# Loading the attention's query tiles ahead, giving out twenty portions of the gate projection first, and padding the compressed values to 128 rows

## The chip, the cores and the metric

The kernel runs on one core of a Trainium2 chip. The metric is the device time of one execution in microseconds (us). Before the change the median of three runs is 1509.44 us (1508.98 to 1510.2). A core has TensorE (PE, matrix products; PEld is its loading of weights), VectorE (DVE), ScalarE (ACT), GpSimd (POOL) and a queue engine (SP) that issues most of the transfers between main memory and the core's own memory.

## The reference

One layer of a decoder with parallel mixers, on 1024 positions of width 1024, all float32:

```python
h = rms_norm(x, norm_mix)
proj = h @ w_in
q_flat, kv_flat, g_attn, u_pool, g_merge = split(proj, ...)
a = nsa_attention(q_flat, kv_flat, g_attn, ...) @ w_branch_attn
b = pool_mixer(u_pool, pool_w, pool_scale) @ w_branch_pool
ga, gb = split(sigmoid(g_merge), 2)
x = x + (ga * a + gb * b) @ w_out
h = rms_norm(x, norm_mlp)
return rms_norm(x + square(relu(h @ w_ff1)) @ w_ff2, norm_final)
```

The attention has 8 heads of 64 in two groups and three branches: over 63 compressed blocks of keys and values, over selected blocks (all 16 blocks are selected, so this is causal attention over everything), and over a window of 512. The three results are added with a sigmoid gate each.

## The kernel before

**Numbers in two parts.** Every large product is made of three: each operand is split into a rounded part (`hi`) and the rest (`lo`), and `mm3` (lines 74 to 79) issues hi·hi, hi·lo and lo·hi. A weight tile comes by SP into `wraw`, ACT rounds it into `whi`, and POOL or DVE subtracts to get `wlo` (`load`, lines 163 to 184).

**Stages.** First keys, values and queries are projected; the query tiles are written to main memory as `qd`, one per 128 positions. Then the pooling branch and its gate are made (lines 424 to 505; the tiles `gbd` go to main memory). Then comes the attention (from line 508), then the output projections, then a feed-forward part.

**The attention.** It goes through 32 pairs: 8 tiles of 128 positions (`i`), and for each 4 pairs of heads (`hp`). A query tile is loaded by `load_q`, for four heads at a time, and `split_q` turns it by four transposes on PE into `qh` and `ql`. For each pair there are two halves. The first (`units_a`) makes the scores on PE (`psS`), the maximum on DVE, the exponential on ACT, and scales the result (`pS` for the compressed block's 64 columns and the selected ones behind them, `pW` for the window). The second (`units_b`) turns the weights back by transposes (`psT`), two blocks of 128 at a time; ACT rounds them (`ph`), DVE subtracts (`pl`), and PE multiplies with the values into `oacc`. The values of the selected and window branches are `vst`, 128 rows; those of the compressed branch are `vch`, 64 rows, and its product is the last block of each pair. The second half of one pair is woven into the first half of the next.

**What fills PE meanwhile.** Another projection, the gate of the attention branch (`ga_terms`), is cut into 128 portions of one `mm3` (three products of 512 columns, into the one buffer `psG`; eight portions make a tile `z`, and a weight column block `m` serves 16). `advance` gives them out in proportion to the work done:

```python
while given < nterm and given < nterm * done / total:
    next(fill, None)
```

**What sets the order.** The code's order is a wish: a scheduler of the tile framework sets each engine's order from it and from the dependencies, so portions and transposes may stand earlier than where the code writes them. An engine then runs its row in order. Memory of a closed pool is used again, and a tile that lies in it waits for the last reader. The query tiles `qi` lie in the attention's own pool `wkB`, which takes over memory of the pooling stage. Beside this, POOL issues sums of feed-forward weights in main memory, one for each step of the attention's progress.

Of the kernel before, what the change touches and what calls it, by code (L numbers as in the profile page):

```python
# [8 lines left out]
F32 = mybir.dt.float32  # L9
F32R = mybir.dt.float32r  # L10
# [7 lines left out]
P = 128  # L18
# [4 lines left out]
HALF = 512  # L23
NH = 8
DH = 64
NG = 2
NCB = 64
# [22 lines left out]
def build(tc, a, out, dbg=None):  # L50
    nc = tc.nc
# [3 lines left out]
    def f(ap):  # L55
        return ap.bitcast(F32)
# [129 lines left out]
    vk = pool(attn, "vk")  # L186
    vst = [vk.tile([P, NT, NG, P], F32R, name=f"vst{b}") for b in range(2)]
    vch = vk.tile([DH, NG, P], F32R, name="vch")
    kds = vk.tile([P, NG, NCB + S], F32R, name="kds")
    kdw = vk.tile([P, NG, S], F32R, name="kdw")  # L190
    qd = [dram.tile([P, 2 * NH * DH], F32, name=f"qd{t}") for t in range(NT)]
# [89 lines left out]
    with ExitStack() as st:  # L281
# [4 lines left out]
        def compress(kv):  # L286
# [61 lines left out]
            else:  # L348
# [6 lines left out]
                for g in range(NG):  # L355
                    nc.vector.tensor_copy(vch[:, g], f(vh[g * DH:(g + 1) * DH]))

# [63 lines left out]
    blkctx.close()  # L421


    with ExitStack() as st:
# [6 lines left out]
        with ExitStack() as st2:  # L431
# [45 lines left out]
            for m in (3, 2, 1, 0):  # L477
                cur = pool_in(m)
                if prev is not None:
                    pool_mix(*prev)  # L480
                prev = cur
            for m in range(NK):
                if made:
# [27 lines left out]
    with ExitStack() as st:  # L511
        wk = pool(st, "wkB")
# [12 lines left out]
        def ga_terms():  # L525
            for m in range(NK):
                gh, gl = load(cols(a["w_in"], C_GA + m * P, P))
                for hf in range(2):
# [10 lines left out]
                    yield  # L539

        def load_q(i, g):
            qi = wk.tile([P, HALF], F32, name="qi", bufs=2)
            nc.sync.dma_start(qi, qd[i][:, g * HALF:(g + 1) * HALF])
            return qi

# [90 lines left out]
        def units_b(u):  # L636
            i, hp, g, nw, w0 = (u[n] for n in ("i", "hp", "g", "nw", "w0"))
            blocks = [(u["pS"], NCB + b * P, vst[0][:, b, g], P) for b in range(i + 1)]
            blocks += [(u["pW"], b * P, vst[1][:, w0 + b, g], P) for b in range(nw // P)]
            blocks.append((u["pS"], 0, vch[:, g], NCB))  # L640
            o = oacc[:, hp % 2]
# [4 lines left out]
            def tr(gi):  # L646
                bl = groups[gi]
                n = len(bl)
                ps = psT.tile([P, HALF], F32, name="psT").rearrange("p (b e n) -> p b e n", b=2, e=2)
                for j, (src, c0, _, _) in enumerate(bl):  # L650
                    for e in range(2):
                        nc.tensor.transpose(ps[:, j, e], src[e][:, c0:c0 + P], ident)  # L652
                ph = wk.tile([P, 2, 2, P], F32R, name="ph", bufs=3)
                pl = wk.tile([P, 2, 2, P], F32R, name="pl", bufs=3)
                nc.scalar.copy(ph[:, :n], ps[:, :n])  # L655
                nc.vector.tensor_tensor(pl[:, :n], ps[:, :n], f(ph[:, :n]), op=SUB)  # L656
                parts[gi] = (ph, pl)

            def pv(gi):
                ph, pl = parts.pop(gi)  # L660
                for part in (ph, pl):
                    for j, (_, _, v, rows) in enumerate(groups[gi]):
                        nc.tensor.matmul(o, lhsT=v, rhs=part[:rows, j], start=gi == 0 and j == 0 and part is ph,  # L663
                                         stop=2 * gi + j == nb - 1 and part is pl)
# [16 lines left out]

        LAG = 1
        fill = ga_terms()
# [5 lines left out]
        def advance(w):  # L689
            nonlocal done, given  # L690
            done += w
            while given < nterm and given < nterm * done / total:
                next(fill, None)
                given += 1

        qi = load_q(0, 0)
        q = split_q(qi)
        qnext = load_q(0, 1)
        bseq, bw = [], 0
# [42 lines left out]
        dump("oT", oT)  # L742
    psTctx.close()
    attn.close()

# [287 lines left out]
```

## Time and profile before

| | |
|---|---|
| median of three runs | 1509.44 us |
| the profiled execution | 1510.39 us, of it a span of 1508.6 us from the first to the last instruction |
| PE busy in the span | 1451.2 us (96%) |
| DVE, ACT, POOL busy | 66%, 50%, 12% |
| TensorE clock granted, mean | 0.981 |
| the attention | from 341.1 to about 708 us of the span |

All times below are of the profiled execution, in us from the start of its span. PE's times are starts and modelled ends, and products overlap their neighbours; so what a product costs is read from the distance of two starts, not from its length.

### The profile page before, as it was taken

How to read it: one execution, taken by the hardware profiler on the slowest of the kernel's cores; microseconds unless marked ns; L12 is line 12 of the kernel's file. 1: busy time of each engine (PE TensorE's matmuls, PEld its weight loads, DVE VectorE, ACT ScalarE, POOL GpSimd, SP SyncE). 2: the span in 40 equal slices, each digit the busy share in tenths (PEclk: the TensorE clock that was granted, in tenths of full speed). 3: DMA queues.
4: the chain of work that ended last, by engine and by line, in shares of the span. 5: the costliest groups of instructions: out<-in, count | busy, mean ns of one | idle time of the engine just before them, and what ended most of it. 6: DMA issues, size and time to landing. Idle time of an engine off the chain costs nothing.

```text
span 1508.6 us, 20793 instructions
## 1 busy us (share of the span) xinstructions
PE 1451.2 (96%) x7369; PEld 1199.6 (80%) x7369; DVE 1001.3 (66%) x1928; ACT 760.6 (50%) x1561; POOL 187.6 (12%) x238
## 2 busy tenths in 40 slices
PE   8999999997999999999899999999999999999995
PEld 6788888886788878787687888888888888888874
DVE  5693451115888888777648368667897386679974
ACT  4454231115877877765334353674344545754441
POOL 2006323330111111110010100000000000001021
PEclk9999999998999999999999999999999999999997
DMA  8234217875668777867944333333332223332312
GB/s 304 70 99 148 70 49 192 213 191 147 179 162 201 177 184 178 196 157 188 323 136 147 113 91 98 96 93 97 98 98 92 97 86 103 98 98 84 109 53 112
DMA packets 130201, 204.67 MB, mean 136 GB/s; under 512 B 9904, under 2 KB 62896, under 8 KB 129584
## 3 DMA queue, kind: packets, MB, share of 16 engines
q1 hardware_dynamic: 112032, 136.22, 28.8%
q0 software_dynamic: 17920, 67.11, 19.5%
q8 instruction: 58, 0.95, 0.3%
q14 instruction: 47, 0.39, 0.1%
q10 hardware_dynamic: 144, 0.00, 0.0%
HBM read 186.52 MB, written 83.89 MB: 179 GB/s over the span
## 4 chain that ended last, share of the span: by engine, by line
PE 84%; DVE 6%; DMA 5%; ACT 3%; issue 1%; POOL 1%; SPq 0%; POOLq 0%; DVEq 0%; ACTq 0%
PE psm L78 16%; PE psm L77 16%; PE psm L79 16%; PE oacc L663 5%; PE psF L78 5%; PE psF L79 5%; PE psF L77 5%; PE psT L652 4%; PE psS L557 3%; PE psS L558 2%; PE psG L77 2%; PE psG L78 2%; PE psG L79 2%; DMA xt<-in_x 1%; PE psS L560 1%
## 5 line engine op out<-in xcount | busy, mean ns | idle before, releaser
L78 PE MATMUL psm<-mv,whi 128*128 128x512 f32 x896 | 351.5, 392 | 0.0
L79 PE MATMUL psm<-mv,wlo 128*128 128x512 f32 x896 | 351.3, 392 | 0.0
L77 PE MATMUL psm<-mv,whi 128*128 128x512 f32 x896 | 351.2, 392 | 0.0
L82 DVE TENSOR_TENSOR wlo<-wraw,whi 128x512 fp32r<-128x512 f32 x288 | 198.8, 694 | 98.8 <-ACT whi L866 70.2
L866 ACT CAST whi<-wraw 128x512 fp32r<-128x512 f32 x224 | 138.8, 620 | 247.8 <-PE psm L78 185.5
L78 PEld LDWEIGHTS psm<-mv,whi 128*128 128x128 f32 x896 | 168.7, 188 | 37.0
L77 PEld LDWEIGHTS psm<-mv,whi 128*128 128x128 f32 x896 | 168.7, 188 | 36.9
L79 PEld LDWEIGHTS psm<-mv,wlo 128*128 128x128 f32 x896 | 168.7, 188 | 36.6
L179 ACT CAST whi<-wraw 128x512 fp32r<-128x512 f32 x112 | 69.7, 622 | 124.5 <-PE psF L78 58.0
L762 POOL TENSOR_TENSOR sqa<-sqa,sq 128x512 f32<-128x512 f32 x24 | 33.4, 1392 | 734.3 <-ACT sq L758 734.3
L656 DVE TENSOR_TENSOR pl<-psT,ph 128x512 fp32r<-128x512 f32 (+1 forms) x160 | 102.0, 647 | 30.3 <-ACT ph L655 29.0
L655 ACT CAST ph<-psT 128x512 fp32r<-128x512 f32 (+1 forms) x160 | 87.8, 556 | 49.0 <-PE psT L652 47.2
L567 DVE TENSOR_REDUCE nm<-psS 128x1 f32<-128x64 f32 (+8 forms) x192 | 100.0, 540 | 17.2 <-PE psS L560 10.1
L82 POOL TENSOR_TENSOR wlo<-wraw,whi 128x512 fp32r<-128x512 f32 x48 | 65.6, 1368 | 108.1 <-ACT whi L179 88.2
L78 PE MATMUL psF<-xl,whi 128*128 128x512 f32 x192 | 74.7, 389 | 0.0
L77 PE MATMUL psF<-xh,whi 128*128 128x512 f32 x192 | 74.7, 389 | 0.0
L79 PE MATMUL psF<-xh,wlo 128*128 128x512 f32 x192 | 74.7, 389 | 0.0
L568 ACT ACTIVATE pS<-psS,nm 128x64 f32<-128x64 f32 (+8 forms) x128 | 68.0, 533 | 8.8 <-DVE nm L567 8.3
L846 ACT CAST mv<-mt 128x512 fp32r<-128x512 f32 x96 | 59.1, 617 | 20.0 <-DVE mt L844 15.5
L82 DVE TENSOR_TENSOR mv<-mt,mv 128x512 fp32r<-128x512 f32 x96 | 67.3, 708 | 1.1 <-ACT mv L846 0.6
L663 PE MATMUL oacc<-ph,vst 128*128 128x256 f32 x264 | 64.1, 318 | 1.2 <-ACT ph L655 0.9
L652 PE MATMUL psT<-cf,pS 128*128 128x128 f32 x352 | 60.4, 276 | 2.8 <-DVE pS L624 2.6
(242 smaller groups left out, 3034.7 us busy)
## 6 DMA issues: line engine op xcount, KB each, us to landing
wraw<-wsw_ff SPq DMA_DIRECT2D x128, 256.0 KB
wraw<-in_w_ff SPq DMA_DIRECT2D x96, 256.0 KB
wsw_ff<-in_w_ff POOLq DMA_DIRECT2D x16, 1024.0 KB, 9.4
wsw_ff<-wsw_ff POOLq DMA_DIRECT2D x16, 1024.0 KB, 9.3
wraw<-in_w_in SPq DMA_DIRECT2D x40, 256.0 KB
wraw<-in_w_out SPq DMA_DIRECT2D x32, 256.0 KB
xt<-in_x SPq DMA_DIRECT2D x8, 512.0 KB
qd<-q SPq DMA_DIRECT2D x16, 256.0 KB
```

Of the source, the lines that this page charges most:

```text
L77: nc.tensor.matmul(ps, lhsT=sh, rhs=mh, start=first and i == 0, stop=False, skip_group_check=more)
L78: nc.tensor.matmul(ps, lhsT=sh, rhs=ml, start=False, stop=False, skip_group_check=more)
L79: nc.tensor.matmul(ps, lhsT=sl, rhs=mh, start=False, stop=last and i == n - 1, skip_group_check=more)
L82: eng.tensor_tensor(lo, src, f(hi), op=SUB)
L179: nc.scalar.copy(h, v)
L567: nc.vector.tensor_reduce(nm, v, axis=AX.X if flat else AX.XY, op=MAX, negate=True)
L568: nc.scalar.activation(p if flat else p.rearrange("p (a n) -> p a n", a=2), v, AF.Exp, bias=nm, accum_out=sm)
L652: nc.tensor.transpose(ps[:, j, e], src[e][:, c0:c0 + P], ident)
L655: nc.scalar.copy(ph[:, :n], ps[:, :n])
L656: nc.vector.tensor_tensor(pl[:, :n], ps[:, :n], f(ph[:, :n]), op=SUB)
L663: nc.tensor.matmul(o, lhsT=v, rhs=part[:rows, j], start=gi == 0 and j == 0 and part is ph, stop=2 * gi + j == nb - 1 and part is pl)
L866: nc.scalar.copy(hi, raw)
```

## The change

- `vch` gets 128 rows; the lower 64 are set to zero once, at the start, by POOL. The products with it take all 128 rows of `ph` and `pl` instead of 64.
- The query tiles `qi` get a pool of their own, `qp`, opened behind the query projection; it has two buffers, as before. The first two tiles are loaded by code that stands in front of the loop over the pooling branch's gate.
- `advance` gives out 20 portions at its first call, and the other 108 in proportion to the work done.

```diff
-    vch = vk.tile([DH, NG, P], F32R, name="vch")
+    vch = vk.tile([P, NG, P], F32R, name="vch")
+    nc.gpsimd.memset(f(vch[DH:P]), 0.0)
...
+    qctx = ExitStack()
+    qp = pool(qctx, "qp")
+
+    def load_q(i, g):
+        qi = qp.tile([P, HALF], F32, name="qi", bufs=2)
+        nc.sync.dma_start(qi, qd[i][:, g * HALF:(g + 1) * HALF])
+        return qi
...
+            qi = [load_q(0, 0), load_q(0, 1)]
             for m in range(NK):
...
-            blocks.append((u["pS"], 0, vch[:, g], NCB))
+            blocks.append((u["pS"], 0, vch[:, g]))
...
-                        nc.tensor.matmul(o, lhsT=v, rhs=part[:rows, j], ...
+                        nc.tensor.matmul(o, lhsT=v, rhs=part[:, j], ...
...
-        LAG = 1
+        LAG, FIRST = 1, 20
...
-            while given < nterm and given < nterm * done / total:
+            while given < nterm and given < FIRST + (nterm - FIRST) * done / total:
...
-        qi = load_q(0, 0)
-        q = split_q(qi)
-        qnext = load_q(0, 1)
+        q = split_q(qi[0])
+        qnext = qi[1]
```

**Where the first query tile is split.** PE's row at the start of the attention, in the kernel before: `psG` are the gate's portions, `cf,qi` the four transposes of the first query tile, `kds,qh` the first scores.

```order
L79 MATMUL psG<-xh_66,wlo 128x512
L77 MATMUL psG<-xh_67,whi 128x512
L78 MATMUL psG<-xl_75,whi 128x512
L549 MATMUL psT<-cf,qi 128x128 x4
L79 MATMUL psG<-xh_67,wlo 128x512
L77 MATMUL psG<-xh_68,whi 128x512
L78 MATMUL psG<-xl_76,whi 128x512
L79 MATMUL psG<-xh_68,wlo 128x512
L557 MATMUL psS<-kds,qh 128x192
```

In the changed kernel the same transposes stand in PE's row some 530 rows earlier, in the first step of the pooling branch's gate (`plh`, `mxh` are the pooled values):

```order
L77 MATMUL psF<-plh,pwh 128x512
L78 MATMUL psF<-pll,pwh 128x512
L79 MATMUL psF<-plh,pwl 128x512
L554 MATMUL psT<-cf,qi 128x128
L77 MATMUL psF<-mxh,whi 128x512
L554 MATMUL psT<-cf,qi 128x128 x3
L78 MATMUL psF<-mxl,whi 128x512
```

The transposes have moved out of the attention's start; they are the only PE work that went into the stage before.

**Where the twenty portions stand.** PE's row behind the first scores, in the changed kernel: `cf,pS` and `cf,pW` are the transposes of the first pair's weights. Ahead of these rows stand 24 products of the gate, behind them 24 more.

```order
L79 MATMUL psG<-xh_71,wlo 128x512
L77 MATMUL psG<-xh_72,whi 128x512
L78 MATMUL psG<-xl_80,whi 128x512
L79 MATMUL psG<-xh_72,wlo 128x512
L657 MATMUL psT<-cf,pS 128x128 x2
L657 MATMUL psT<-cf,pW 128x128 x2
L562 MATMUL psS<-kds,qh 128x192
L563 MATMUL psS<-kds,ql 128x192
L77 MATMUL psG<-xh_65,whi 128x512
```

In the kernel before the transposes of the first pair follow straight on the scores of the second:

```order
L557 MATMUL psS<-kdw,qh 128x128
L558 MATMUL psS<-kdw,ql 128x128
L652 MATMUL psT<-cf,pS 128x128 x3
L652 MATMUL psT<-cf,pW 128x128 x2
L652 MATMUL psT<-cf,pS 128x128
```

Up to the first pair's product with `vch` stand 6 portions before, and 22 now. In the 25 pairs behind it the counts are the same in both (88 portions). So the portions that moved to the front are missing in the last six pairs: 33.7 before, 17.7 now.

**The last pair.** PE's row at the end of the attention, in the kernel before:

```order
L652 MATMUL psT<-cf,pW 128x128 x4
L78 MATMUL psG<-xl_79,whi 128x512
L79 MATMUL psG<-xh_71,wlo 128x512
L663 MATMUL oacc<-ph,vst_98 128x256 x2
L663 MATMUL oacc<-pl,vst_98 128x256 x2
L652 MATMUL psT<-cf,pW 128x128 x2
L652 MATMUL psT<-cf,pS 128x128 x2
L77 MATMUL psG<-xh_72,whi 128x512
```

and in the changed kernel:

```order
L657 MATMUL psT<-cf,pW 128x128 x4
L668 MATMUL oacc<-ph,vst_98 128x256 x2
L668 MATMUL oacc<-pl,vst_98 128x256 x2
L657 MATMUL psT<-cf,pW 128x128 x2
L657 MATMUL psT<-cf,pS 128x128 x2
L668 MATMUL oacc<-ph,vst_98 128x256 x2
```

Nothing of the gate is left between the last pair's steps.

## Rows read from the trace of the kernel before

**Rows 1.** The page: busy time, share of the span and instructions of each engine.

```profile
PE 1451.2 (96%) x7369; PEld 1199.6 (80%) x7369; DVE 1001.3 (66%) x1928; ACT 760.6 (50%) x1561; POOL 187.6 (12%) x238
```

**Rows 2.** Busy us by engine, granted clock, DMA: first pair, next 25, last six.

```profile
341.10:361.90 20.80, 15.31 (x75) 12.66 (x75) 7.92 (x34) 8.17 (x34) 1.02 (x1) 0.75 0.48 128
361.90:618.50 256.60, 251.42 (x1648) 202.85 (x1647) 210.59 (x513) 199.86 (x524) 42.03 (x47) 1.00 0.74 180
618.50:708.20 89.70, 87.95 (x569) 72.76 (x568) 69.75 (x133) 62.91 (x132) 12.06 (x14) 1.00 0.72 168
```

**Rows 3.** Who waited for whom on PE, whole span: total, times, longest.

```profile
PE psT L549 <- DMA qi<-qd: 4.6, 1, 4.6
...
PE psm L79 <- DVE wlo L82: 2.7, 1, 2.7
```

**Rows 4.** Order of time, PE at the attention's start: start, length, instruction, idle before.

```profile
342.86 0.39 PE L78 MATMUL psG<-xl,whi 128*128 128x512 f32 x1
347.85 1.12 PE L549 MATMUL psT<-cf,qi 128*128 128x128 f32 x4 [4.60 <-DMA qi<-qd]
```

**Rows 5.** Order of time, SP's queue: pool weights, then the first query tile.

```profile
162.29 0.39 SPq L435 DMA_DIRECT2D s<-in_pool_w  x1
...
340.32 0.44 SPq L543 DMA_DIRECT2D qi<-qd  x1
```

**Rows 6.** Busy us by engine, then granted clock, behind the wait for the query tile.

```profile
345.00:352.00 7.00, 4.15 (x17) 3.73 (x17) 1.15 (x3) 0.78 (x2) 0.00 (x0) 0.53 0.75 257
352.00:359.00 7.00, 6.14 (x34) 5.18 (x34) 5.21 (x27) 5.90 (x29) 0.00 (x0) 0.74 0.00 1
```

**Rows 7.** Busy us of the gate's portions alone (PE, PEld, DVE): same stretches.

```profile
341.10:361.90 20.80, 8.15 (x21) 4.87 (x21) 0.00 (x0) 0.75 0.48 128
361.90:618.50 256.60, 85.94 (x264) 44.34 (x263) 7.52 (x11) 1.00 0.74 180
618.50:708.20 89.70, 31.84 (x100) 16.65 (x100) 3.42 (x5) 1.00 0.72 168
```

**Rows 8.** Order of time, PE: ordinary products of 128 rows, in the middle.

```profile
480.11 0.28 PE L663 MATMUL oacc<-ph,vst 128*128 128x256 f32 x1
480.23 0.40 PE L663 MATMUL oacc<-pl,vst 128*128 128x256 f32 x2
...
481.14 0.39 PE L77 MATMUL psG<-xh,whi 128*128 128x512 f32 x1
481.37 0.40 PE L78 MATMUL psG<-xl,whi 128*128 128x512 f32 x1
```

**Rows 9.** Order of time, PE: one product of 64 rows between products of 128.

```profile
548.59 0.29 PE L663 MATMUL oacc<-ph,vst 128*128 128x256 f32 x1
548.81 0.38 PE L663 MATMUL oacc<-ph,vch 64*128 64x256 f32 x1
549.12 0.50 PE L77 MATMUL psG<-xh,whi 128*128 128x512 f32 x1
549.46 0.39 PE L78 MATMUL psG<-xl,whi 128*128 128x512 f32 x1
```

**Rows 10.** Order of time, PE: two products of 64 rows side by side.

```profile
442.52 0.38 PE L663 MATMUL oacc<-ph,vch 64*128 64x256 f32 x1
442.75 0.27 PE L663 MATMUL oacc<-pl,vch 64*128 64x256 f32 x1
442.95 0.50 PE L77 MATMUL psG<-xh,whi 128*128 128x512 f32 x1
443.29 0.40 PE L78 MATMUL psG<-xl,whi 128*128 128x512 f32 x1
```

**Rows 11.** Busy us of the products with `vch` (PE, PEld, DVE): same stretches.

```profile
341.10:361.90 20.80, 0.50 (x2) 0.29 (x2) 0.00 (x0) 0.75 0.48 128
361.90:618.50 256.60, 15.41 (x50) 8.14 (x50) 0.00 (x0) 1.00 0.74 180
618.50:708.20 89.70, 4.06 (x12) 2.05 (x12) 0.00 (x0) 1.00 0.72 168
```

More of the change, by code (lines that the diff above doesn't have):

```diff
@@ L355, in compress @@
                 for g in range(NG):
-                    nc.vector.tensor_copy(vch[:, g], f(vh[g * DH:(g + 1) * DH]))
+                    nc.vector.tensor_copy(vch[0:DH, g], f(vh[g * DH:(g + 1) * DH]))
         def keys(t, br, dst):
@@ L539, in ga_terms @@
                     yield
[L541 to L544, printed above, removed]
         def split_q(qi):
@@ L637, in units_b @@
             i, hp, g, nw, w0 = (u[n] for n in ("i", "hp", "g", "nw", "w0"))
-            blocks = [(u["pS"], NCB + b * P, vst[0][:, b, g], P) for b in range(i + 1)]
-            blocks += [(u["pW"], b * P, vst[1][:, w0 + b, g], P) for b in range(nw // P)]
-            blocks.append((u["pS"], 0, vch[:, g], NCB))
+            blocks = [(u["pS"], NCB + b * P, vst[0][:, b, g]) for b in range(i + 1)]
+            blocks += [(u["pW"], b * P, vst[1][:, w0 + b, g]) for b in range(nw // P)]
+            blocks.append((u["pS"], 0, vch[:, g]))
             o = oacc[:, hp % 2]
@@ L649, in tr @@
                 ps = psT.tile([P, HALF], F32, name="psT").rearrange("p (b e n) -> p b e n", b=2, e=2)
-                for j, (src, c0, _, _) in enumerate(bl):
+                for j, (src, c0, _) in enumerate(bl):
                     for e in range(2):
@@ L661, in pv @@
                 for part in (ph, pl):
-                    for j, (_, _, v, rows) in enumerate(groups[gi]):
-                        nc.tensor.matmul(o, lhsT=v, rhs=part[:rows, j], start=gi == 0 and j == 0 and part is ph,
+                    for j, (_, _, v) in enumerate(groups[gi]):
+                        nc.tensor.matmul(o, lhsT=v, rhs=part[:, j], start=gi == 0 and j == 0 and part is ph,
                                          stop=2 * gi + j == nb - 1 and part is pl)
@@ L743, in build @@
     psTctx.close()
+    qctx.close()
     attn.close()
```

## The prediction

> **What bounds the kernel now.** I read the page's busy times first [rows 1]: PE is busy 96% of the span, the others at most 66%. So an edit counts for what it takes from PE's row, and for what it lets PE wait. Only the attention is touched. Its three stretches [rows 2] are the first pair, the 25 pairs behind it and the last six. In the middle PE is busy 251.4 of 256.6 us and in the last stretch 87.95 of 89.7; DVE, the next, has 82% and 78%. So PE is the bound there, with DVE not far behind. In the first stretch PE is busy only 15.3 of 20.8 us. The list of waits [rows 3] names the reason: 4.6 us for the first query tile, the longest wait there but for small ones on DVE and ACT.
>
> Busy isn't the same as useful, though, because products overlap. What one costs is the distance to the next start. An ordinary 128-row product of 256 columns takes 0.12 us (480.11 to 480.23), one of 512 columns 0.23 us (481.14 to 481.37) [rows 8]. A portion, three of the latter, is 0.69 us of PE.
>
> **Part 1, the query tile and the portions at the front.** Now the load goes out at 340.32, when SP comes to it [rows 5], and PE stops: starts at 342.86 and 347.85, 4.99 us apart where 0.23 would do, so 4.8 us lost [rows 4]. Then the granted clock is 0.53 and 0.74 in the next two stretches of 7 us [rows 6], so partly the lower level of 1.2 GHz instead of 2.4, after that stop and a sparse row of PE. The work done in 4.15 and 6.14 busy us would have taken 4.15 x 0.47 + 6.14 x 0.26 = 3.5 us less at the full level.
>
> After the change the load stands behind the query projection, about 180 us earlier, and the transposes stand in the pooling gate's first step, so the wait goes. What is late next is the rounding of `qh` and `ql` on ACT and DVE; one portion's product and some 0.5 us of waiting lie there, a small part of the rest below. The load takes SP's place in front of the pool weights [rows 5]; both wait for the same release of memory, and nothing queued behind them is needed within the microsecond that two more issues take. I cost that at nothing; if that cover fails, it is about 1 us. The added memset on POOL at the start is also nothing: POOL is 12% busy.
>
> The first stretch now holds 20.8 us = 4.8 of waiting + 3.5 of low clock + 7 portions (21 products in [rows 7]) of 0.69 = 4.8 + a rest of 7.7, in which PE also waits for the softmax of the first pair. PE's row after the change has 22 portions up to the same point: 15.2 us. The rest lies between 5 us (all its waits covered) and 7.7. I take 6.8 less 0.4 for the first pair's share of part 2: 21.6 us, +0.8 us. The bounds are -1 and +2. So the stretch stays as long, but takes 15 portions more with it.
>
> **Part 2, the padding.** The third timeline [rows 9] shows one product with the 64-row `vch`: the product ahead of it takes 0.22 instead of 0.12 us, it takes 0.31 instead of 0.12, and the 512-column one behind it 0.34 instead of 0.23. That is 0.10 + 0.19 + 0.11 = 0.40 us for one excursion to 64 rows. Two side by side [rows 10] take 0.23 and 0.20 and the one behind 0.34, which is 0.30, and with 0.10 for the one ahead again 0.40. There are 64 such products, 2, 50 and 12 by stretch [rows 11]. By PE's row, 18 pairs have their two side by side and 14 have them apart, so 18 + 28 = 46 excursions: 1 in the first stretch, 35 in the middle, 10 in the last. At 0.40 us that is 14.0 us in the middle and 4.0 in the last. A padded product is an instruction like the one with `vst`, and I take 0.12 us for it.
>
> The Trainium skill is of two minds here. "TensorE: Matmul & The Clock Gate" says under "What happens when you issue a matmul" that the time of a weight load goes by its columns and that the row count doesn't matter; by that the padding would change nothing, which is the second rival below. "TensorEngine Tiling (Array Packing)" says under "Key Properties" that a change of tiling mode drains the array, and 64 rows are such a mode; the delays on both sides of the 64-row product agree with this one.
>
> How much of it stays? In the middle nothing else changes: the same 88 portions stand in it. 256.6 - 14.0 = 242.6 us would put DVE, with 210.6 us of work, at 87%; it is at 82% now, while PE is the bound. I take 86% as what it reaches before PE loses time to it, so 210.6 / 0.86 = 244.9 us: **-11.7 us**. The bounds are -14.0 and, if DVE couldn't go over 82%, nothing.
>
> **Part 3, the last six pairs.** 16 portions fewer (33.7 against 17.7 by PE's rows; the 100 products in [rows 7] agree), 16 x 0.69 = 11.0 us, and 4.0 us of part 2: PE needs 74.7 us. DVE's 69.75 us lose two evictions of the gate (3.42 us for 5), so 68.4 us. That would be 92%; at 86% the stretch takes 79.5 us: **-10.2 us**. The bounds are -15.0 (no time lost to DVE) and 68.4 / 0.82 = 83.4 us, -6.3.
>
> **Behind the attention** nothing is edited, but it starts some 20 us earlier, with the same transfers in a shorter time (DMA share 0.72 to 0.74 now [rows 2]). PE waits there once for 2.7 us for a late weight tile [rows 3]; that wait may go or double, so 3 us either way, taken as 0.
>
> **Sum.** 0.8 - 11.7 - 10.2 = -21.1 us. The profiled execution took 1510.39 us, which gives 1489.3. The median of the runs lies 0.95 us under that execution, so **1488 us**.
>
> **The rivals.**
> - *DVE takes over.* PE waits little on DVE now only because PE is slow enough; with less fill between the steps of a pair, DVE's 82% is the ceiling. Against it: PE is busy for 98% of the middle, so the 82% is what PE leaves it. For it: the last pairs lose their fill altogether. Then the middle gains nothing and the last stretch 6.3: 0.8 - 6.3 = -5.5, 1504 us. Chance 14%.
> - *The padding does nothing*, that is, the delays belong to `vch`'s place at the end of a pair and not to its rows. For it: it is always the last block. Against it: also the product behind is late, where it is a gate portion that waits for nothing. Then 1.2 in front, 0 in the middle, and the last stretch's PE work is 78.7 us, still under 79.5 at 86%: -10.2. Together -9.0, 1500 us. Chance 7%.
> - *Slower: the last six pairs fall apart.* Without portions, transposes, rounding, subtraction and product of a pair follow each other, and PE and DVE work by turns. PE has 74.7 us there and DVE 68.4. The other parts give 10.9 us, so this decides, with 3 us more for a measurable loss, from the point where the stretch takes over 89.7 + 13.9 = 103.6 us: when 42% of DVE's work lies outside PE's. At half it is 108.9 us, +19.2 - 10.9 = +8.3 us: 1518 us. Against it: two `psT` buffers and the next pair's scores still overlap. Chance 4%.
>
> **How the numbers follow.** The forecast has 75%, the rivals 14, 7 and 4%. The range takes in the lowest sum (-1 - 14 - 15 = -30, 1479; with the part behind one way or the other it is rarely reached, so 1480) and reaches up to the second rival's 1500, at 1501; what is outside is most of the first and all of the third rival. A measurement of this kernel tells 0.2%, 3 us, from no change. Faster by more: the forecast, the second rival and nearly all of the first, 92%; within: a mixture of the first and third, 4%; slower: 4%.
>
> **What would show it.** In the profile after: no wait of PE for `qi`, and the granted clock at 1 from 341 us on; the first pair's end still at about 362 us. A `vch` product with a start distance of about 0.12 us, and its neighbours at theirs. The middle stretch at about 245 us with DVE at 86%, the last at about 80 us, PE waiting there for DVE or ACT. Wrong would be: a middle that is no shorter (first or second rival, told apart by the distances at `vch`), a last stretch over 90 us, or a front that is longer by several microseconds because PE waits for `qh` or for the portions' weights.

## The result, and the profile after

The changed kernel takes 1501.05 us (median of 6 runs, 1498.78 to 1505.85) against 1510.05 us for the kernel before on the same chip (6 runs, 1508.98 to 1511.78). The ratio is 0.9936, with a 95% interval of 0.992 to 0.9952: 9 us faster, 0.6%. The forecast was 22 us. The sign was right and the size was not: the time lies at the very top of the range, 0.05 us outside, and less than half of the forecast gain came.

The profiled execution has a span of 1497.0 us. First the page's busy times, which answer to [rows 1]:

```profile
PE 1439.9 (96%) x7369; PEld 1193.7 (80%) x7369; DVE 1001.6 (67%) x1928; ACT 760.4 (51%) x1561; POOL 188.9 (13%) x239
```

PE has 11.3 us less work, and its share is still 96%. The three stretches of [rows 2], now from 337.2 us on, with the same columns (busy us of PE, weight loads, DVE, ACT and POOL, then granted clock and DMA):

```profile
337.20:359.70 22.50, 21.61 (x120) 17.83 (x121) 9.72 (x35) 9.86 (x37) 3.56 (x3) 1.00 0.44 119
359.70:609.50 249.80, 243.82 (x1651) 199.89 (x1648) 211.28 (x513) 199.75 (x523) 42.77 (x47) 1.00 0.76 184
609.50:695.80 86.30, 78.80 (x520) 65.35 (x519) 68.21 (x132) 61.44 (x129) 9.87 (x12) 0.98 0.72 165
```

| stretch | before | forecast | after |
|---|---|---|---|
| first pair | 20.8 | 21.6 | 22.5 |
| next 25 pairs | 256.6 | 244.9 | 249.8 |
| last six pairs | 89.7 | 79.5 | 86.3 |
| the three together | 367.1 | 346.0 | 358.6 |

The attention lost 8.5 us. Behind it the kernel takes 0.8 us more. The stretch ahead of it is 3.9 us shorter in this execution, but that isn't the change: from 55 to 62 us the trace of before has a granted clock of 0.52, and this one has 1.00. The traces of the experiments show that dip in most cases and not in others, whatever the edit: of two executions of one and the same kernel, e3 has it and e9 has not.

The portions alone, as in [rows 7]: 22 in the first pair, 89 in the middle, 17 in the last six.

```profile
337.20:359.70 22.50, 16.38 (x66) 12.08 (x66) 1.38 (x2) 1.00 0.44 119
359.70:609.50 249.80, 84.39 (x266) 45.02 (x266) 7.48 (x11) 1.00 0.76 184
609.50:695.80 86.30, 16.25 (x52) 8.96 (x52) 2.06 (x3) 0.98 0.72 165
```

Two `vch` products side by side, in order of time on PE, at the place of [rows 10] (start, length, instruction):

```profile
437.15 0.48 PE L668 MATMUL oacc<-pl,vst 128*128 128x256 f32 x2
437.46 0.28 PE L668 MATMUL oacc<-ph,vch 128*128 128x256 f32 x1
437.58 0.28 PE L668 MATMUL oacc<-pl,vch 128*128 128x256 f32 x1
437.70 0.39 PE L77 MATMUL psG<-xh,whi 128*128 128x512 f32 x1
437.93 0.40 PE L78 MATMUL psG<-xl,whi 128*128 128x512 f32 x1
```

The distances are 0.12, 0.12 and 0.23 us, where [rows 10] has 0.23, 0.20 and 0.34: at this place the padding removed the 0.30 us that the prediction read there, and 0.09 more ahead of it. So the instructions became as fast as forecast. PE's waits within the attention (total, times, longest):

```profile
PE psT L657 <- DVE pS L629: 6.0, 9, 1.1
PE oacc L668 <- DVE pl L661: 2.7, 10, 0.5
PE psS L562 <- ACT pS L573: 1.7, 1, 1.7
PE oacc L668 <- ACT ph L660: 1.2, 3, 0.5
```

The 4.6 us for the query tile [rows 3] are gone. What is there instead is the pair itself: transposes that wait until DVE has scaled `pS`, products that wait for `pl`, scores that wait until ScalarE has read the last ones.

### The profile page after: what moved, and what is told of

Its sections match the earlier page's. It is cut to its first block, busy times and chain, and to the rows that moved or that the text cites. A ratio compares the mean times of both kernels' runs of the same rounds, so it can differ in the third digit from the quotient of the medians.

```text
span 1497.0 us, 20789 instructions
## 1 busy us (share of the span) xinstructions
PE 1439.9 (96%) x7369; PEld 1193.7 (80%) x7369; DVE 1001.6 (67%) x1928; ACT 760.4 (51%) x1561; POOL 188.9 (13%) x239
## 4 chain that ended last, share of the span: by engine, by line
PE 84%; DVE 8%; DMA 3%; ACT 3%; issue 1%; POOL 1%; SPq 0%; POOLq 0%; DVEq 0%; ACTq 0%
PE psm L78 16%; PE psm L77 16%; PE psm L79 16%; PE psF L78 5%; PE oacc L668 5%; PE psF L77 5%; PE psF L79 5%; PE psT L657 4%; PE psS L562 3%; PE psS L563 2%; PE psG L77 2%; PE psG L78 2%; PE psG L79 2%; DMA ta<-tad 1%; PE psS L565 1%
## 5 line engine op out<-in xcount | busy, mean ns | idle before, releaser
L179 ACT CAST whi<-wraw 128x512 fp32r<-128x512 f32 x112 | 69.7, 622 | 126.6 <-PE psF L78 56.9
L82 DVE TENSOR_TENSOR mv<-mt,mv 128x512 fp32r<-128x512 f32 x96 | 67.2, 707 | 1.1 <-ACT mv L851 0.6
```

What stands on the lines that cost most here:

```text
L82: eng.tensor_tensor(lo, src, f(hi), op=SUB)
L179: nc.scalar.copy(h, v)
```

## The experiments

All compare with the kernel before, measured beside them; there it took 1513.6 to 1514.3 us and not 1510, so the ratios are what to compare, not the times. Two theories went in. **A**: a pair has a length of its own, from the scores over maximum, exponential, scaling, transpose, rounding and subtraction to the products. PE's time saved below that length comes back as waits, and portions in it are free. **B**: DVE's throughput is the ceiling. A third, **C**, was that the padding does nothing. This table is worked out from the traces: portions are products of the gate by three, and the stretches end as those above do, where DVE begins the last addition of a pair's result (`oT`).

| kernel | portions | first pair | middle | last six | ratio, 95% interval |
|---|---|---|---|---|---|
| before | 7 / 88 / 33 | 20.8 | 256.6 | 89.7 | 1 |
| padding alone (e1) | 7 / 88 / 33 | 22.3 | 250.8 | 87.8 | 0.9940 (0.9925 to 0.9955) |
| tile ahead alone (e11) | 3 / 93 / 32 | 10.5 | 267.5 | 86.7 | 0.9975 (0.9964 to 0.9986) |
| tile ahead, 20 first (e2) | 22 / 89 / 17 | 22.5 | 256.9 | 90.7 | 0.9979 (0.9967 to 0.9990) |
| tile ahead, padding (e3) | 3 / 93 / 32 | 10.6 | 258.6 | 84.6 | 0.9908 (0.9894 to 0.9922) |
| the same again (e9) | 3 / 93 / 32 | 10.5 | 258.3 | 84.5 | 0.9910 (0.9893 to 0.9928) |
| tile ahead, padding, 8 first (e4) | 10 / 91 / 27 | 14.8 | 254.1 | 89.1 | 0.9931 (0.9913 to 0.9949) |
| the change: all, 20 first | 22 / 89 / 17 | 22.5 | 249.8 | 86.3 | 0.9936 (0.9920 to 0.9952) |
| the change again (e10) | 22 / 89 / 17 | 22.6 | 249.3 | 86.3 | 0.9922 (0.9906 to 0.9939) |

A kernel's stretches repeat to half a microsecond (e3 and e9, the change and e10).

One thing in the table misleads. At the end of the middle DVE's addition starts about 1 us behind the end of PE's last product in the other kernels of the table, but 4.2 to 5.5 us behind it in e3, e9 and e11, where it stands in DVE's queue behind work for later pairs. In e3 (start, length, instruction):

```profile
602.98 0.28 PE L668 MATMUL oacc<-pl,vch 128*128 128x256 f32 x1
608.72 0.28 DVE L674 TENSOR_TENSOR oT<-oacc,ot 64x128 f32<-64x128 f32 x1
```

So the table makes the middle of these three 3 to 4 us too long against the others, and their last six as much too short. Cut at the end of PE's last product of a pair instead, the middle and the last six are:

| kernel | portions, middle / last six | middle | last six |
|---|---|---|---|
| before | 88 / 33 | 256.9 | 89.9 |
| e1 | 88 / 33 | 251.1 | 88.0 |
| e11 | 90 / 35 | 264.8 | 90.4 |
| e2 | 89 / 17 | 257.5 | 90.9 |
| e3 | 90 / 35 | 255.2 | 89.0 |
| e9 | 90 / 35 | 255.9 | 87.8 |
| the change | 89 / 17 | 250.4 | 86.7 |

### Padding alone

```diff
-    vch = vk.tile([DH, NG, P], F32R, name="vch")
+    vch = vk.tile([P, NG, P], F32R, name="vch")
+    nc.gpsimd.memset(f(vch[DH:P]), 0.0)
...
-            blocks.append((u["pS"], 0, vch[:, g], NCB))
+            blocks.append((u["pS"], 0, vch[:, g], P))
```

> Padding alone. Theory A (the padding gives PE its 0.40 us per excursion, but the pairs hand part of it back in waits; the last pairs are bound by the length of their chain once they have no fill): the middle 25 pairs about 7 us shorter, as in the changed kernel, the last six pairs 2 to 4 us shorter because their portions are still there to fill the gaps; 1499 to 1502 us. Rival B (DVE is the ceiling of the middle at 82%): the middle stays at 256 us and the whole within 1508 to 1511. Rival C (the padding does nothing, the middle's gain in the changed kernel came from somewhere else, such as the clock or the order of the front): 1510, each vch product still 0.2 to 0.3 us.

Measured: ratio 0.9940, 1503.74 us. Its middle and last six, in the columns of [rows 2]:

```profile
359.90:610.70 250.80, 243.34 (x1647) 199.49 (x1646) 211.62 (x512) 200.08 (x523) 43.47 (x47) 1.00 0.76 184
610.70:698.60 87.90, 85.64 (x568) 71.71 (x567) 69.57 (x135) 63.04 (x133) 12.16 (x14) 1.00 0.74 169
```

C falls, and so does B in its strict form: the middle got 5.8 us shorter and DVE went from 82% to 84%. A had 7 us for the middle and 2 to 4 for the last six, where 1.9 came. The first pair got 1.5 us longer, since PE waits 6.3 us for the query tile here and not 4.6. This kernel's PE row stands in the same order as before's, so start distances can be compared instruction by instruction. In the middle the `vch` products with their neighbours on both sides take 10.7 us less. All the other instructions there take 5.0 us more: the transposes of `pS` 2.3 us, the products with `pl` 1.5, the scores most of the rest. 10.7 won on the spot, 5.0 handed back. The waits of PE in the middle show the same two names growing, before first (where `pl` has no row) and then with the padding:

```profile
PE psT L652 <- DVE pS L624: 2.0, 3, 1.1
```

```profile
PE psT L653 <- DVE pS L625: 2.9, 4, 1.1
PE oacc L664 <- DVE pl L657: 1.7, 2, 1.3
```

Over the whole kernel the excursions of which both traces have all records (46) gave 14.8 us on the spot, 0.32 us each in the mean (0.38 in the median) and not 0.40.

### The front without the padding

The changed kernel with the four lines on `vch` put back and `rhs=part[:v.shape[0], j]` in the product.

> The query tile ahead and twenty portions first, without the padding. Theory A: the first pair's stretch 22 to 23 us, 1 to 2 us longer than before; the middle unchanged at 256 us; the last six pairs, with 16 portions fewer, only 0 to 3 us shorter because the last pairs wait for their own chain: 1508 to 1511 us. Rival B (DVE throughput): the last six pairs get down to what DVE needs at 82 to 86%, 80 to 83 us, so 1502 to 1505. Rival C: the whole gain of the change is here, 1501.

Measured: 0.9979, 1511.57 us. The first pair's stretch is 22.5 us. The last six:

```profile
621.10:711.80 90.70, 84.67 (x521) 68.92 (x520) 68.38 (x132) 61.53 (x129) 9.19 (x12) 0.94 0.71 160
```

Here 16 portions, 11 us of PE's work, were taken out of a stretch in which PE was busy for 88 of 89.7 us [rows 2], and it became 1.0 us longer. Part of it is the clock: 10.2 us of the stretch ran at 0.50, where before has 1.00 throughout, so up to 5.1 us were lost that way. Even without them the stretch would have gained 4 us at most, and not 11. That refutes the third part of the prediction. Theory A's numbers hold but for this stretch, which it had 0 to 3 us shorter.

### Fewer portions first

```diff
-        LAG, FIRST = 1, 20
+        LAG, FIRST = 1, 0
```

(and 8 in the second kernel.)

> The changed kernel with no portions given out first (query tile ahead and padding stay); by PE's row 2.7 portions stand in the first pair, 90.5 in the middle and 35 in the last six. Theory A: a portion in front costs nearly its full 0.69 us there, and one in the last pairs costs nearly nothing, so without them the front takes 10 to 14 us instead of 22.5, the middle 251, the last six 86 to 88: 1491 to 1497 us, faster than the changed kernel. Rival B or C: the portions in front only fill its gaps; without them the front still takes 18 to 20 us and the last six pairs are back at 88 to 90: 1500 to 1504 us, no better than the changed kernel.

> The changed kernel with eight portions first instead of twenty: 10 in the first pair, 89.7 in the middle, 28.4 in the last six by PE's row. Theory A: front 14 to 17 us, middle 250 to 251, last six 85 to 87, so 1493 to 1498 us, between the kernel without any portions first and the changed one. Rival B or C: front 18 to 20, last six 84 to 88: 1499 to 1503 us.

Measured: 0.9908 (1500.44 us) and 0.9931 (1503.17 us). The kernel with none first:

```profile
339.50:350.10 10.60, 9.51 (x65) 7.55 (x65) 7.94 (x34) 7.78 (x34) 0.95 (x1) 1.00 0.95 211
350.10:608.70 258.60, 249.10 (x1669) 205.15 (x1668) 212.70 (x517) 201.88 (x526) 42.18 (x47) 0.99 0.74 179
608.70:693.30 84.60, 82.82 (x555) 69.87 (x554) 66.94 (x130) 60.83 (x130) 12.26 (x14) 1.00 0.73 172
```

In front A is right: 10.6, 14.8 and 22.5 us with 3.3, 10 and 22 portions, so a portion there costs 0.64 us. In the last six it is nearly right, cut at PE's last product: 35 portions and 89.0 us (87.8 in e9) against 17 and 86.7 in the changed kernel, so 18 portions, 12 us of PE's work, cost 1 to 2 us. But the middle was to be as long as the changed kernel's, and cut so it is 4.8 us longer. One or two portions more (0.9 us) and one stretch of low clock (at most 1.7) don't cover that. The rest goes with where the portions stand: in the last five pairs of the middle e3 has 27 and the changed kernel 20.7, and there e3 takes 69.7 us and the changed kernel 65.1. In the 20 pairs ahead of them e3 has 5 portions fewer, 3.4 us of PE's work, and is no shorter (185.5 and 185.3 us, with the low clock in it). So a portion can cost its full price in one pair and bring little when it is missing from another. With eight first the last six have 89.1 us at a clock of 0.96; there the forecast missed.

### No portions in the pairs

```diff
-        LAG, FIRST = 1, 20
+        LAG, FIRST = 1, 128
```

> The changed kernel with all 128 portions given out first, so that the last 25 pairs or so have no fill at all: what a pair takes when only its own chain and engines bound it. Theory A (the late pairs are bound by their chain): the last six pairs take as long without any of the changed kernel's 17 portions, 83 to 88 us, plus what a low granted clock adds, and 7-2 and 7-3 again 16 to 18 and 10 to 12 us; with 88 portions moved out of the middle, it gets shorter by much less than 88 x 0.69 = 60 us: 30 to 45, and the whole kernel is slower than the changed one, 1510 to 1535 us. Rival B' (PE's work bounds the pairs also without fill): the middle falls by 55 to 60 us, the last six to 75 to 78, the whole stays within 1495 to 1505 us.

Measured: 1567.07 us, ratio 1.034. All portions stand in the pairs of the first row of queries, up to 447.1 us. The 22 pairs behind them, and the last six:

```profile
447.10:678.40 231.30, 195.91 (x1299) 155.54 (x1298) 188.73 (x456) 176.86 (x453) 24.45 (x32) 0.97 0.65 156
678.40:762.60 84.20, 71.12 (x468) 57.18 (x466) 65.04 (x126) 57.84 (x123) 9.57 (x12) 0.96 0.65 153
```

The same 22 pairs with 83 portions in them, in the changed kernel, and in the kernel before:

```profile
375.30:609.50 234.20, 229.84 (x1553) 188.56 (x1551) 197.80 (x463) 187.41 (x476) 41.21 (x45) 1.00 0.77 187
```

```profile
377.70:618.50 240.80, 237.11 (x1552) 191.67 (x1551) 197.77 (x466) 187.89 (x479) 40.47 (x45) 1.00 0.74 180
```

This is the view that was missing ahead of the prediction. 83 portions are 57 us of PE's work, and the pairs took 3 us longer with them. Without any of them the last six take 84.2 us, 2.1 less than with 17. Some of that is the clock: without portions 13.7 us of the 22 pairs and 6.8 of the last six ran at 0.50, in the changed kernel none and 3.4. At the full clock the 22 pairs would be up to 6.8 us shorter, and their 83 portions would then cost 10 us, still a sixth of their work. Without portions PE is busy for 85 and 84% of these stretches, and waits (total, times, longest, from 447 us on) for the same things as in the changed kernel, only more:

```profile
PE psT L657 <- DVE pS L629: 11.1, 18, 1.5
PE oacc L668 <- DVE pl L661: 10.1, 28, 0.9
PE psS L562 <- ACT pW L573: 8.1, 12, 1.4
PE psS L562 <- ACT pS L573: 5.8, 5, 2.6
PE oacc L668 <- ACT ph L660: 4.9, 14, 0.6
```

Five of the 22 pairs, 5-1 to 6-1, ran at the full clock in all of these kernels. Here they are, cut at PE's last product, without portions (e5), with 20.7 (the changed kernel) and with 27 (e3):

```profile
613.70:677.10 63.40, 56.15 (x374) 43.25 (x374) 52.74 (x105) 47.05 (x107) 7.64 (x10) 1.00 0.73 174
543.30:608.40 65.10, 64.45 (x439) 53.30 (x439) 54.36 (x108) 50.46 (x114) 12.96 (x14) 1.00 0.83 194
533.60:603.30 69.70, 68.33 (x459) 57.17 (x458) 54.47 (x109) 50.67 (x113) 9.75 (x12) 1.00 0.74 180
```

The first 20.7 portions cost 1.7 us, 0.08 each. The next 6.3 cost 4.6 us, 0.73 each, which is their full price. The repeats e10 and e9 have 64.9 and 69.6 us. (PE's row differs in its order between the three too, not by the portions alone.)

The kernel as a whole was slower than A expected, because moving the portions costs their full price in front and gives back next to nothing: A was right in kind and still too timid. Put together for the 28 pairs behind the first row: 315 us with no portion, 320 with 100 (the changed kernel), 324 with 116 (e1), 329 with 120 (e3). Up to about 100 a portion costs 0.05 us (0.13 if all the low clock was lost time), above it 0.2 and more. PE's work and the pairs' own length meet about there, and the kernel before, with 116, stood only a little beyond. That fits with how close the kernels of the table lie.

### What the pairs' length is made of

Six kernels tried to tell. Three have no portions first: the first leaves out the gate's multiplication on DVE, the second scales `pS` in two pieces, the third writes products two groups behind their transposes.

```diff
-                    nc.vector.tensor_tensor(z, ps, rB[:, sl], op=MUL)
-                    nc.scalar.activation(z, z, AF.Tanh, scale=0.5)
+                    nc.scalar.activation(z, ps, AF.Tanh, scale=0.5)
```

> The changed kernel with no portions first, and with the multiplication of the gate by the row scale on DVE left out (16 instructions of 0.68 us, 10.9 us of DVE's work; ScalarE takes its tanh from the accumulator instead; the output is without that scale). Those instructions stand in no pair's chain. Rival B (DVE's throughput is the ceiling): middle and last six together 9 to 12 us shorter than the 343 us of the same kernel with the multiplication, so 1488 to 1492 us. Theory A (the chain): 0 to 3 us shorter, 1497 to 1501 us.

```diff
+                cut = NCB + min(ns, 2 * P)
+                for e_ in range(2):
+                    pS = u["pS"][e_]
+                    nc.vector.tensor_scalar(pS[:, NCB:cut], pS[:, NCB:cut], c[:, e_, 1:2], None, op0=MUL)
...
-                    nc.vector.tensor_scalar(pS[:, NCB:NCB + ns], pS[:, NCB:NCB + ns], c[:, e_, 1:2], None, op0=MUL)
+                    if cut < NCB + ns:
+                        nc.vector.tensor_scalar(pS[:, cut:NCB + ns], pS[:, cut:NCB + ns], c[:, e_, 1:2], None, op0=MUL)
```

> The changed kernel with no portions first, and with the scaling of pS on DVE cut in two, the first 256 columns of both heads ahead of the rest, so that a pair's first transposes can start some 1 us earlier; DVE's work grows by two instructions a pair (some 0.1 us each). Theory A: the waits of the transposes for pS (6 us in the changed kernel, and 2.3 us of what the padding gave back) mostly go, 2 to 5 us shorter, 1495 to 1498 us. Rival B (DVE throughput): no gain, or 1 to 5 us longer by the added instructions, 1500 to 1505 us.

```diff
-        LAG, FIRST = 1, 20
+        LAG, FIRST = 2, 0
```

> The changed kernel with no portions first, and with a pair's products written two groups behind their transposes instead of one, so that rounding on ScalarE and subtraction on DVE have a group more of PE's work to hide behind. Theory A in the form that the step from transposes to products is the chain's tight part: the waits of products for pl and ph go (4 us in the changed kernel), 1495 to 1498 us. If the tight part is the softmax ahead of the transposes, or DVE's throughput: no gain, 1499 to 1503 us.

Measured: 0.9879 (0.9858 to 0.9899), 0.9918 (0.9898 to 0.9938) and 0.9908 (0.9888 to 0.9929). Cutting the scaling gained nothing, and neither did the longer lag: A's form in which one step is the tight part fails twice. But the scheduler also set the rest of PE's row anew in each of the three (tile by tile, some 85% of e3's row stands in the same order in e6 and e7), so none is a change of one step alone. Taking 10.9 us of work off DVE took 4.4 us out of the middle and 0.2 out of the last six. Up to 1.7 of it is the stretch of low clock that e3 has there and e6 has not, so it lies near A's 3 and is at most half of B's 9 to 12; its interval and that of e3 overlap slightly.

The other three have all portions in front, as e5. A multiplication (128x1024, 0.75 us) was added to DVE, or a copy of that size (1.16 us) to ScalarE, once a pair, dependent on the pair's own maximum and read by nobody; the third cuts the scaling. Each of the three was executed once.

```diff
+            if e == 0:
+                dm = wk.tile([P, S], F32, name="dm", bufs=1)
+                nc.vector.tensor_scalar(dm, rB, u["nm"][:, 0, 2:3], None, op0=MUL)
```

```diff
+                nc.scalar.activation(dm, rB, AF.Copy, scale=u["nm"][:, 0, 2:3])
```

> All portions ahead of the pairs, and on DVE one multiplication of 128x1024 a pair (0.75 us) whose result nobody reads. Against the same kernel without it: 231.2 us from the end of pair 0-3 to the end of 6-1 (22 pairs) and 84.2 for the last six. If DVE's queue is the floor, each pair gets longer by its 0.75 us: 22 x 0.75 = 16.5 and 6 x 0.75 = 4.5 us. If it is the chain or ScalarE, the addition goes into DVE's idle fifth: 0 to 5 and 0 to 1.5 us.

> All portions ahead of the pairs, and on ScalarE one copy of 128x1024 a pair (about 1.1 us by the scalings and exponentials of that size) that nobody reads. If ScalarE's queue is the floor: 22 x 1.1 = 24 and 6 x 1.1 = 6.6 us longer; if DVE's queue or the chain: 0 to 8 and 0 to 2 us.

> All portions ahead of the pairs, and the scaling of pS cut in two, the first 256 columns of both heads first. If the length of the chain from the softmax to the transposes is the floor, some 1 us a pair is gained where pS is long (from row 2 on): 10 to 20 us on the 22 pairs and 3 to 6 on the last six. If a queue's load is: nothing, or 0.1 to 0.2 us a pair lost, 2 to 4 us.

The 22 pairs and the last six, of the kernel with more work on DVE, then of that with more on ScalarE, then with the cut scaling (e5 has 231.3 and 84.2):

```profile
447.80:687.80 240.00, 204.22 (x1298) 164.17 (x1298) 202.52 (x476) 178.03 (x453) 25.18 (x32) 0.92 0.63 151
687.80:774.60 86.80, 73.95 (x468) 59.66 (x467) 68.01 (x131) 57.83 (x123) 9.60 (x12) 0.92 0.65 150
```

```profile
449.60:690.90 241.30, 202.54 (x1303) 160.88 (x1303) 190.92 (x455) 200.61 (x476) 25.79 (x32) 0.95 0.63 151
690.90:781.20 90.30, 74.41 (x460) 59.97 (x460) 64.37 (x126) 62.35 (x128) 9.51 (x12) 0.91 0.61 142
```

```profile
446.50:676.50 230.00, 196.45 (x1299) 155.66 (x1298) 193.05 (x491) 177.38 (x453) 25.17 (x32) 0.98 0.66 158
676.50:760.30 83.80, 70.74 (x468) 58.28 (x467) 66.14 (x139) 58.60 (x123) 9.62 (x12) 0.94 0.64 151
```

With DVE the pairs got 8.8 and 2.6 us longer for 16.4 and 3.7 us of work, with ScalarE 10.1 and 6.1 for 25.5 and 5.7 (of the added instructions 22 and 5 stand in these stretches). That is between what either expectation said, but the clock is in it. In the 22 pairs 37.5 us ran at 0.50 with the work on DVE, 23.9 with that on ScalarE and 13.7 in e5, so up to 11.9 of the 8.8 us and 5.1 of the 10.1 can be PE's low clock; in the last six up to 3.4 of the 2.6 and 5.1 of the 6.1. How much the queue itself counts is therefore not shown. What is shown is that the added work did not lengthen the pairs by its whole length, so neither queue was full, and that the cut gained 1.3 and 0.4 us of the 10 to 20 and 3 to 6 that the scaling would have given as the single tight step. The account that is left is a loop over three engines whose queues run in order. What exactly closes it in which pair stays open.

### The parts again, and two that take work off DVE

> The changed kernel with no portions first, beside the changed kernel itself on one chip. What the runs so far say (a portion in the pairs costs next to nothing, one in front of them 0.64 us): 3 to 6 us below the changed kernel; if the difference between the two earlier runs was one of chips, within 2 us of it.

> The changed kernel again, for comparison on this chip: 3 to 6 us above the one without portions first, ratio to before 0.993 to 0.995.

Measured on one chip: 0.9910 without portions first and 0.9922 with twenty, 1.6 us apart. The expected 3 to 6 us were not there. The earlier two ratios differ by 0.3%, these by 0.1%, and their intervals overlap: twenty portions first cost between nothing and 4 us, and bring nothing.

> The query tile ahead alone: no portions first, no padding. Theory (wait of 4.8 us and the low clock behind it are all that it removes, and nothing gives it back): the first pair's stretch 11 to 13 us with 3.3 portions instead of 22 with 7, of which 3.7 portions, 2.5 us, have only moved on; 5 to 8 us faster than before, ratio 0.9945 to 0.997. Rival (what the front gains, the pairs give back, since they are bound by their own chain and now start with less done): within 3 us of before.

That kernel is e2 with `FIRST` at 0. Measured: 0.9975, 1509.19 us, so 0.25% or 4 us. Its first two stretches:

```profile
339.90:350.40 10.50, 9.51 (x64) 7.50 (x65) 7.91 (x33) 7.79 (x34) 1.02 (x1) 1.00 0.66 165
350.40:617.90 267.50, 259.50 (x1670) 208.55 (x1670) 212.18 (x518) 201.46 (x527) 42.31 (x47) 0.99 0.74 174
```

By the table the front gained 10.3 us (2.5 of them by 3.7 portions that moved on) and the last six 3.0, and the middle lost 10.9. Cut at PE's last product, the front gained 10.7 us, the middle lost 7.9 and the last six 0.5. At most 1.7 of that is a stretch of low clock. 5.3 lie in the last five pairs of the middle (72.5 us with 27 portions against 67.2 with 20.7). The other 20 pairs are 2.7 us longer although they have nearly 5 portions fewer. Both theories had a part: the wait and the low clock behind it did go, and most of that came back in the pairs.

```diff
-                    nc.vector.tensor_tensor(z, ps, rB[:, sl], op=MUL)
+                    nc.scalar.copy(z, ps)
+                    nc.gpsimd.tensor_tensor(z, z, rB[:, sl], op=MUL)
```

> The changed kernel with no portions first, and with the gate's multiplication by the row scale moved from DVE to GpSimd (ScalarE copies the accumulator out first, 16 x 0.6 us more for it); everything is computed. If DVE's in-order queue is part of the pairs' chain, as the 4 us of the run without that multiplication hint: 2 to 5 us below the one without portions first. If ScalarE's queue is as much a part of it, or GpSimd's transfers hold its result back: no gain or a few us longer.

Measured: 0.9937 (0.9921 to 0.9952), 1503.62 us, no gain but 3 us more than e9. DVE lost the multiplications, but ScalarE got as many copies.

The last three move the scaling of the 64 compressed columns to GpSimd, without any work for ScalarE, with 0, 20 and 8 portions first:

```diff
-                    nc.vector.tensor_scalar(pS[:, :NCB], pS[:, :NCB], c[:, e_, 0:1], None, op0=MUL)
+                    nc.gpsimd.tensor_scalar(pS[:, :NCB], pS[:, :NCB], c[:, e_, 0:1], None, op0=MUL)
```

> The changed kernel with no portions first, and with the scaling of the 64 compressed columns of pS moved from DVE to GpSimd (two instructions of 0.25 us a pair, 16 us of DVE's work in all; they are needed only by a pair's last transposes). If taking work off DVE is worth half, as adding is: some 4 to 8 us below the kernel without portions first, 1493 to 1497 us, ratio to before 0.985 to 0.989. If GpSimd's transfers, behind which the scaling queues, hold a pair's last transposes back: as slow as that kernel or slower, 0.991 or more.

> The same with twenty portions first as in the changed kernel; by PE's row 22 portions in the first pair, 82 in the middle and 24 in the last six. If the pairs hold some 100 portions for nothing and the front takes 0.64 us for each: within 3 us of the kernel without portions first, since what the front costs the middle gains; the middle 243 to 248 us.

> The same with eight portions first: 10, 88 and 30 portions. By the same reasoning the best of the three by 1 to 4 us: front 15 to 17, middle 247 to 252, last six 82 to 85.

Measured: 0.9899 (0.9881 to 0.9917), 0.9936 (0.9915 to 0.9958) and 0.9886 (0.9868 to 0.9903). The first gained 1 us and not 4 to 8 over the one with DVE doing it. The second was no better than the changed kernel; its middle took 253.0 us, with 82 portions and one stretch of low clock (at most 1.7), and not 243 to 248. The third has the lowest ratio of those that compute everything: 1496.81 us, its interval just below both intervals of the changed kernel (from 0.9906 on), but overlapping those of e3, e9 and the first.

```profile
339.70:354.10 14.40, 12.76 (x81) 10.92 (x82) 8.18 (x30) 8.07 (x34) 2.49 (x5) 1.00 0.57 147
354.10:607.80 253.70, 247.93 (x1648) 203.99 (x1646) 204.03 (x466) 200.46 (x525) 71.34 (x97) 0.99 0.74 182
607.80:693.60 85.80, 83.23 (x559) 69.39 (x557) 67.34 (x121) 62.09 (x131) 20.15 (x25) 1.00 0.73 173
```

Each stretch misses what was expected of it by 0.6 to 1.7 us. It takes 8 us out of the front against the changed kernel, and pays 4 of them in the middle. Which of the two edits, and how much the particular order that the scheduler made of it, gave the rest was not separated.

## Why the prediction was right in sign and wrong in size

**The query tile.** Right: no wait for `qi`, and a granted clock of 1.00 in the first stretch. The stretch came to 22.5 us, within the bounds that the prediction gave but 0.9 over its value. A portion there costs 0.64 us, a little less than the 0.69 assumed; the rest is 22.5 - 22 x 0.64 = 8.4 us and not 6.4 (6.8 less the padding's 0.4). What the prediction did not ask is what it is worth to end the first pair early: by e11, most of it comes back in the middle.

**The padding.** The mechanism was right: in the same place, with 128 rows, the products are fast, so it was the rows. The Trainium skill's "TensorEngine Tiling (Array Packing)" says under "Key Properties" that a change of tiling mode drains the array; the delays on both sides of the 64-row product agree with that. The Trainium skill's sentence in "TensorE: Matmul & The Clock Gate" under "What happens when you issue a matmul", that the row count doesn't matter, is about the load of the weights. There the trace of before agrees: 0.18 us with 64 rows, 0.19 with 128. It doesn't follow that padding changes nothing, since 64 rows among 128 cost 0.3 to 0.4 us around the load. Two sizes were off. The 35 excursions of the middle gave 10.7 us and not 14.0, as 0.40 was read at places without a wait nearby. And 5.0 of these were handed back, against the 2.3 that "DVE reaches 86%" allowed for. In the changed kernel DVE reached 84.6%, at 249.8 us. The step that failed here is the ceiling of 86%: it was chosen, not read. PE's waits for single steps of a pair (the scaled `pS`, `pl`) had grown while DVE was still idle for 15% of the time; what exactly sets that point stays open.

**The last six pairs.** This is the step that failed in kind. The prediction read "PE is the bound there" from a PE that was busy for 87.95 of 89.7 us, and so took 16 x 0.69 = 11.0 us off PE's work and off the time. But the pairs take nearly as long without that work: cut at PE's last product, 84.7 us with no portion (e5), 86.7 with 17 (the changed kernel) and 88.0 with 33 (e1), of which the low clock has up to 3.4, 1.7 and 0. The 3.4 us that were gained are the padding's share there (1.9 in e1) and 1.5 for the 16 portions. DVE did not come near the 86% either: it stands at 77 to 79% in all three. The rival "DVE takes over" had 82% and 83.4 us for that stretch, and came nearest; its middle, with no gain, was wrong. The rival by which the padding does nothing had 1500 us, a microsecond from the result, and is wrong all the same: its time came from a gain in the last six that wasn't there.

The chain can be read where the portions have run out, in the changed kernel at the end of pair 7-1 (start, length, instruction, idle before it):

```profile
666.66 1.36 DVE L572 TENSOR_REDUCE nm<-psS 128x1 f32<-128x1024 f32 x2 [0.52 <-PE psS L565]
668.10 1.11 ACT L573 ACTIVATE pS<-psS,nm 128x1024 f32<-128x1024 f32 x1
669.36 0.41 PE L562 MATMUL psS<-kdw,qh 128*128 128x320 f32 x1 [1.75 <-ACT pS L573]
671.46 0.74 DVE L629 TENSOR_SCALAR pS<-pS,cc 128x1024 f32<-128x1024 f32 x1
672.26 0.44 PE L657 MATMUL psT<-cf,pS 128*128 128x128 f32 x2 [0.53 <-DVE pS L629]
```

The next scores can't start before the maximum (1.36 us, with a small second one in the row) and the exponential (1.11) have read the ones before, and the transposes can't before the scaling (0.74) is done. PE stands still for 1.75 and 0.53 us. In the kernel before 33 portions stood in the last six pairs, and PE looked full.

**The clock.** "At 1 from 341 us on" was wrong at one place of the attention. Pair 7-2 of the changed kernel has no portion, and a dip follows:

```profile
668.40:685.20 16.80, 12.67 (x85) 9.96 (x86) 13.82 (x30) 12.36 (x27) 2.05 (x2) 1.00 0.72 163
686.00:689.40 3.40, 3.38 (x14) 3.16 (x15) 1.58 (x3) 1.04 (x2) 0.51 (x1) 0.50 1.11 312
```

PE worked for 12.67 of 16.8 us, and then ran at 0.50, the lower of its two levels, for 3.4 us. The last six of e2 and e5 have such dips too; those of before, e1 and e3, with 33 to 35 portions, have none. So taking portions away can also cost clock, a second reason why it gave so little. But portions are no guarantee: the last six of e4, with 27, had 6.8 us at 0.50, and the middle of e3, with 90, had 3.4.

**Behind the attention.** 0.8 us longer, inside the 3 us either way. The wait for a late weight tile grew as the prediction allowed, from 2.7 us [rows 3] to 3.8:

```profile
PE psm L79 <- DVE wlo L82: 3.8, 1, 3.8
```

**The sum.** Forecast 0.8 - 11.7 - 10.2 = -21.1 us; measured 1.7 - 6.8 - 3.4 = -8.5 in the attention. Of the 12.6 us that are missing, 6.8 are the last six, 4.9 the middle and 0.9 the front. By parts: the padding is worth 0.6%, the tile ahead 0.25%, the twenty portions first nothing or a small loss.

## What to carry to other kernels

An engine that is busy for 98% may be filled up and not the bound: when a scheduler puts independent work into the gaps, ask how long the stretch takes without that work, for instance by moving all of it elsewhere once, before anything taken off the engine is counted as time. Filler in gaps is nearly free up to the point where both lengths meet (about 100 portions in 28 pairs here), so it should stay where the gaps are; put ahead of them it costs its full price. And a percentage of another engine at which it "becomes the bound" should be read from a run in which it does, since here the loop over three engines closed at 77 to 85% of DVE.

## What the runs showed of the hardware that was not expected

- An odd operand among like ones: one 64-row weight tile between 128-row ones cost 0.32 us on the spot in the mean of 46 places (0.38 in the median), in the product ahead, in itself and in the product behind, and padding it with zeros took that away at no price in PE's instructions (0.12 us each).
- In the pairs with no filler the granted clock fell to 0.50 for 3.4 or 6.8 us at a time, in stretches in which PE was busy for 75 to 85% of the time.
- A scaling of 128x64 that takes 0.25 us on DVE took 0.43 to 1.67 us on GpSimd (median 0.67 to 0.74), and the kernels with it there were no slower.
